# The low parts of the scores in zero-padded tiles of 128 rows

## The chip, the cores and the metric

The kernel runs on one NeuronCore of a Trainium2 chip. The metric is the device time of one execution in microseconds (us). TensorE is called PE below, and its weight loads PEld; VectorE is DVE, ScalarE is ACT, GpSimd is POOL, and SyncE is SP. A difference of 0.2% (2.3 us) is about what a measurement of this kernel can tell from none.

## The reference, cut to what matters

One layer of a hybrid encoder over 512 tokens of 2048 features, all in float32. Half of the mixing heads are differential attention, the other half retention.

```python
u = rmsnorm(h, attn_norm)                    # h: 512 x 2048
z = u @ w_in                                 # 2048 x 7168
rq, rk, rv, rg, dq, dk, dv, dg = split(z)
# retention: 8 heads, keys of 64 features, values of 128
ro = retention(rope(rq), rope(rk) * 64**-0.5, rv)     # (q k^T * decay) v
ro = rmsnorm(ro, ret_gn) * silu(rg)
# differential attention: 8 heads, two scores of 64 features each, values of 128
dq, dk = rmsnorm(dq, diff_qn), rmsnorm(dk, diff_kn)
do = (softmax(q0 k0^T) - lam * softmax(q1 k1^T)) @ dv  # causal by chunks of 64
do = rmsnorm(do, diff_subln) * 0.8 * silu(dg)
h = h + concat(ro, do) @ w_out
out = h + sigmoid(rmsnorm(h, ple_norm) @ w_ple_gate) * (p @ w_ple_proj)
```

## The kernel before, in words

Activations lie feature-major: 128 features on the partitions, 512 tokens in the free dimension. Every float32 operand of a product is split exactly into a high and a low part of type float32r, x = hi + lo, and a product is carried as hi\*hi + hi\*lo + lo\*hi, that is as three matmuls into the same accumulator (`mm3`, L113 to L115). The high part is made by ACT (L106, L109), the low part by DVE (L107, L110).

The projections are cut into chunks of 256 output columns. A chunk goes through 16 k-blocks of 128 features, two k-blocks at a time; such a step is called a slice below. A slice of a feature-major chunk (`fm_products`) has 12 matmuls of 512 columns, one of a values chunk (`v_products`) 24 of 256 columns. A slice is a tick of a clock that the program keeps while it is traced. What follows from a chunk (norms, scores, transposes, values) is set into an agenda some ticks ahead (`after`, `queue_ret`, the tables `QK`, `SCORES`, `TURNS`, `VALUES`, `NORMS`, `RET`), so that these small steps stand between slices of projection products in PE's order. A scheduler then fixes the order of each engine from the traced order and priorities.

**Scores of differential attention** (`stack_q`, `stack_k`, `diff_steps.scores`). A head has two scores of 64 features each. For the first, `qa` holds the high part of q in rows 0 to 63 and its low part in rows 64 to 127, and `k0` holds the high part of k in both halves; one matmul with 128 rows gives hi\*hi + lo\*hi. The remaining term, high part of q by low part of k, is a second matmul into the same bank that takes 64 rows alone: `qs[half, c]` by `kl[half, :L]`. `kl` holds the low part of the first score's k in rows 0 to 63 and that of the second in rows 64 to 127. The second score uses `qb`, `k1` and the other half. For query block b the products have L = 128 (b + 1) columns, so a group of four matmuls (two scores, two products each) has 128, 256, 384 or 512 columns. There are 8 heads of 4 blocks: 32 such groups.

**Scores of retention** (`q_done`, `k_done`, `ret_steps.scores`). `ks` holds the high part of k in one half and the low part in the other, `qd` the high part of q in both; the last term takes the 64 rows of `ks` with the high part and `ql[half]`. A call does two key blocks, of 512 and 384 or of 256 and 128 columns. There are 8 heads of two calls: 16 groups of four matmuls.

In both places every second matmul has 64 rows: 64 at L389 and 32 at L529. `kl` lies in a pool with two buffers, `ql0` and `ql1` in one with a single buffer, a tile for two heads. `squares2` (the squares of a head's output for its norm) takes its tiles for retention from the pool `tmp`, which lives for the whole kernel; the pools `rp` and `rc` live only for the retention stage, and the pool `mixp` (the split operands `mh`, `ml` of the output projection) is opened behind them.

Of the kernel before, what the change touches and what calls it, by code (L numbers as in the profile page):

```python
# [12 lines left out]
F32 = mybir.dt.float32  # L13
# [5 lines left out]
P = 128  # L19
S = 512  # L20
# [18 lines left out]
def f(ap):  # L39
    return ap.bitcast(F32)  # L40
# [3 lines left out]
def tile_layer(  # L44
# [14 lines left out]
):  # L59
    """out^T of one layer.  # L60

    Activations are kept feature-major ([features, tokens]); every product of the
    projections is carried by float32r operands that split float32 exactly into
    x = hi + lo, as hi*hi + hi*lo + lo*hi.
    """
    nc = tc.nc
# [12 lines left out]

# [1 line left out]
    nc.scalar.preload_act_table_set(NORM_SET)  # L81
# [21 lines left out]
    def split(hi, lo, src, gain=None):  # L103
        """hi + lo = src * gain exactly, both float32r."""
        if gain is None:
            nc.scalar.activation(hi, src, AF.Copy)  # L106
            nc.vector.tensor_tensor(lo, src, f(hi), ALU.subtract)  # L107
        else:
            nc.scalar.activation(hi, src, AF.Copy, scale=gain)  # L109
            nc.vector.scalar_tensor_tensor(lo, src, gain, f(hi), ALU.mult, ALU.subtract)  # L110
# [5 lines left out]

# [1 line left out]
    def wchunk(wd, n0, nk, name):  # L118
# [13 lines left out]
    def fm_products(acc, k, nk, wh, wl, mh, ml):  # L132
        """One k-block of [256 features, 512 tokens]: out^T += W^T m."""
        for j in range(2):
            c = slice(j * P, (j + 1) * P)
            mm3(acc[j], wh[:, c], wl[:, c], mh[k], ml[k], k == 0, k == nk - 1)
# [3 lines left out]
    def v_products(acc, k, wh, wl):  # L140
        """One k-block of values of two heads: two [128, token block, 256]."""
        for t in range(4):
            c = slice(t * P, (t + 1) * P)
            o = acc[t // 2][:, (t % 2) * CW:(t % 2 + 1) * CW]
            mm3(o, u_hi[k][:, c], u_lo[k][:, c], wh, wl, k == 0 and t % 2 == 0, k == KB - 1)

    # A job is a generator that traces one slice (two k-blocks) of a chunk's products
    # at a time and, at its end, the evacuation.  An evacuation sets the steps that
    # follow from it some slices ahead, so that the tensor engine has products to do
    # while the other engines prepare a step's operands.  # L150
    agenda = defaultdict(list)
# [49 lines left out]
    def rsqrt(y, z, ss, scale):  # L201
        """y ~ (ss*scale)^-0.5; returns z so that y*(z + 1.5) is it to float32."""
        nc.scalar.activation(y, ss, AF.Ln, scale=scale)
        nc.scalar.activation(y, y, AF.Exp, scale=-0.5)
        nc.scalar.activation(z, y, AF.Square)
        nc.vector.scalar_tensor_tensor(z, ss, -0.5 * scale, z, ALU.mult, ALU.mult)
# [34 lines left out]

    def squares2(src, eps2, name, pool=tmp):
        """As squares, of features in pairs: the low parts lie below the high ones."""
        lo, hi = slice(0, 64), slice(64, P)
# [10 lines left out]
    def normed(t, sq, sel, width, tag, name, cut=None):  # L255
        """t *= rsqrt(mean of squares + eps) over the blocks of sel, 0 where the sum reaches cut."""
        z, sh, sl = sq
# [10 lines left out]

# [1 line left out]
    with ExitStack() as st:  # L270
        xp = st.enter_context(tc.tile_pool(name="xp", bufs=1))
        ssum = xp.tile([P, S], F32, name="ssum")

        # The first two chunks together, a k-block at a time as x arrives; until then
        # products of ones keep the tensor engine's clock up.
        warm = bank("tp", 1, "warm")
# [32 lines left out]

    # lam = exp(lq1.lk1) - exp(lq2.lk2) + 0.2.  The differential output is carried  # L310
    # scaled by c = 1 / max(1, |lam|); its norm undoes the scale.
    lsum = const.tile([P, 2], F32, name="lsum")
# [17 lines left out]
    nc.vector.tensor_scalar(eps_d, eps_d, 2.0**-62, 2.0, ALU.max, ALU.mult)  # L330
    # The reference's sum of squares overflows, and its rsqrt is 0, from here on.
    thr = const.tile([P, 1], F32, name="thr")
# [11 lines left out]

    # ---- differential attention, two heads at a time; on_d holds the gates, then the
    # gated outputs ----
    on_d = [onp.tile([P, S], F32, tag=f"ond{h}", name=f"ond{h}") for h in range(8)]
    A0, A1 = slice(0, 64), slice(64, 128)

    with ExitStack() as st:  # L350
        dp = st.enter_context(tc.tile_pool(name="dp", bufs=2))

        def stack_q(t, h):
# [8 lines left out]
        def stack_k(t, h):  # L362
            k0 = dp.tile([P, S], F32R, tag="k0", name=f"k0{h}")
            k1 = dp.tile([P, S], F32R, tag="k1", name=f"k1{h}")
            kl = dp.tile([P, S], F32R, tag="kl", name=f"kl{h}")
            nc.scalar.activation(k0[A0], t[A0], AF.Copy, scale=g_dk[A0])
            nc.scalar.activation(k1[A1], t[A1], AF.Copy, scale=g_dk[A1])
            nc.vector.tensor_copy(k0[A1], f(k0)[A0])
            nc.vector.tensor_copy(k1[A0], f(k1)[A1])
            nc.vector.scalar_tensor_tensor(kl[A0], t[A0], g_dk[A0], f(k0)[A0], ALU.mult, ALU.subtract)  # L370
            nc.vector.scalar_tensor_tensor(kl[A1], t[A1], g_dk[A1], f(k1)[A1], ALU.mult, ALU.subtract)
            return k0, k1, kl

        def diff_steps(h, pair):
            """Steps of one head: scores and softmax, transposes, values, norm."""
            own = {}
            j = h % 2

            def scores(b):
                qa, qb = pair["q", j]  # L380
                k0, k1, kl = pair["k", j]
                L = (b + 1) * P
                c = slice(b * P, (b + 1) * P)
                sts = small.tile([P, 4], F32, tag="sts", name=f"sts{h}_{b}")
                pt = [dp.tile([P, S], F32, tag=f"p{i}", name=f"p{i}_{h}_{b}") for i in range(2)]
                for i, (qs, ks, half) in enumerate(((qa, k0, A0), (qb, k1, A1))):
                    sc = bank("sc", 2, f"sc{h}_{b}_{i}")[:, :L]
                    nc.tensor.matmul(sc, lhsT=qs[:, c], rhs=ks[:, :L], start=True, stop=False)
                    nc.tensor.matmul(sc, lhsT=qs[half, c], rhs=kl[half, :L], start=False, stop=True)  # L389
                    nc.vector.memset(sc[A0, L - 64:L], NEG)  # L390
# [97 lines left out]

# [1 line left out]
    onr_pool = ctx.enter_context(tc.tile_pool(name="onr", bufs=1))  # L490
    on_r = [onr_pool.tile([P, S], F32, tag=f"onr{h}", name=f"onr{h}") for h in range(8)]

    with ExitStack() as st:
# [20 lines left out]
        def ret_steps(h, qkv):  # L514
            own = {}
            (qd, ql, half), ks = qkv["q", h], qkv["k", h]
            vh, vl = qkv["v"]
            hc = slice((h % 2) * P, (h % 2 + 1) * P)

            def scores(k0):  # L520
# [3 lines left out]
                for kb in (k0, k0 + 1):  # L524
# [3 lines left out]
                    nc.tensor.matmul(sc[:, :N], lhsT=ks[:, c], rhs=qd[:, kb * P:], start=True, stop=False)  # L528
                    nc.tensor.matmul(sc[:, :N], lhsT=ks[half, c], rhs=ql[half, kb * P:], start=False, stop=True)  # L529
                    sf = rp.tile([P, S], F32, tag="sf", name=f"sf{h}_{kb}")  # L530
# [6 lines left out]
            def values(k0):  # L537
# [7 lines left out]
                if k0:  # L545
                    nc.scalar.activation(on_r[h], o, AF.Copy)
                    own["sq"] = squares2(on_r[h], eps2, f"r{h}")

# [14 lines left out]
        for g in range(2):  # L563
            qkv = {}

            def q_done(acc, g=g, qkv=qkv):
                for j in range(2):
                    t = rope(acc[j], f"q{g}_{j}")
                    ql = rc.tile([P, S], F32R, tag=f"ql{j}", name=f"ql{g}_{j}")
                    for i, (half, oth) in enumerate(((A0, A1), (A1, A0))):  # L570
                        qd = rc.tile([P, S], F32R, tag=f"qd{j}{i}", name=f"qd{g}_{j}{i}")
                        nc.scalar.activation(qd[half], t[half], AF.Copy)
                        nc.vector.tensor_copy(qd[oth], f(qd)[half])
                        nc.vector.tensor_tensor(ql[half], t[half], f(qd)[half], ALU.subtract)
                        qkv["q", 4 * g + 2 * j + i] = qd, ql, half

# [30 lines left out]

# [1 line left out]
    mixp = ctx.enter_context(tc.tile_pool(name="mixp", bufs=1))  # L609
# [18 lines left out]

# [1 line left out]
    h_hi, h_lo, h_sb = [], [], []  # L630
    ssum = small.tile([P, S], F32, name="ssum2", bufs=1)

# [20 lines left out]

# [1 line left out]
    p_hi, p_lo = [], []  # L655
# [30 lines left out]
    def output(b, ag, pp, c):  # L686
        """Tokens c of the 128 features of block b; ag holds just those."""
        n = c.stop - c.start
# [14 lines left out]

    # The last chunk a block at a time, its second block by halves of the tokens: less
    # is left to do after the last product.
    pp = ple(7, (("tp", 1), ("o", 1)))
# [20 lines left out]
def _tables():  # L727
    """Rotary cosines and sines and retention decays: they depend on shapes alone."""
    pos = np.arange(S, dtype=np.float32)
# [47 lines left out]
```

## Time and profile before

| | |
|---|---|
| median of 3 runs | 1132.52 us (1132.52 to 1132.53) |
| profiled execution, first to last instruction | 1130.5 us |
| its own time beside the span | as the runs: about 2.0 us lie outside the span |
| PE busy | 1119.7 us (99%), 5668 matmuls |
| PEld busy | 934.6 us (83%), 5668 loads |
| DVE busy | 650.3 us (58%), 1206 instructions |
| ACT busy | 570.1 us (50%), 1049 instructions |
| POOL busy | 0.7 us, 6 instructions |
| DMA | 111.21 MB, 98 GB/s over the span |

The span runs from the first to the last instruction of the program on the core. Busy times are unions of the instructions' durations. Matmuls overlap in the records (a matmul of 512 columns is shown with 389 ns, and the next one starts some 227 ns after it), so PE's busy share does not tell how densely it is fed: for that, the starts of successive matmuls are read from the timeline, and the time from one start to the next is called an interval below. PEclk is the granted clock of TensorE as a share of 2.4 GHz.

### The profile page before, as it was taken

The page shows a single profiled execution, that of the slowest core. Times are in us where ns is not written, and L with a number is a line of the kernel's source. Part 1 is how long each engine was busy: PE and PEld are TensorE (multiplying, and loading weights), DVE is VectorE, ACT ScalarE, POOL GpSimd, SP SyncE. Part 2 cuts the span into 40 slices and gives each one's busy share as a digit, 9 for nine tenths or more (in the row PEclk, how much of TensorE's full clock was granted, in tenths as well). Part 3 has the DMA queues.
Part 4 walks back from the last instruction along what each step waited for, and adds up shares of the span by engine and source line. Part 5 has one row for each costly group of instructions (what it writes and reads, how often), then busy time and mean ns, then how long its engine had stood idle before and what let it go on. Part 6 is the DMA issues. An engine that isn't in the chain of part 4 may idle for free.

```text
span 1130.5 us, 14883 instructions
## 1 busy us (share of the span) xinstructions
PE 1119.7 (99%) x5668; PEld 934.6 (83%) x5668; DVE 650.3 (58%) x1206; ACT 570.1 (50%) x1049; POOL 0.7 (0%) x6
## 2 busy tenths in 40 slices
PE   9999999999999999999999999999999999999998
PEld 7887788788878887899779988888888888888887
DVE  8577579548754875476675467643353354333442
ACT  8467576657665755654575368533333344222230
POOL 0000000000000000000000000000000000000000
PEclk9999999999999999999999999999999999999999
DMA  7422221222222222232222223543332333333341
GB/s 245 127 84 91 75 76 60 74 73 81 87 74 75 76 81 69 88 119 88 90 84 76 89 80 93 186 150 110 95 93 94 96 106 106 112 116 127 109 142 39
DMA packets 104631, 111.21 MB, mean 98 GB/s; under 512 B 4464, under 2 KB 97008, under 8 KB 104560
## 3 DMA queue, kind: packets, MB, share of 16 engines
q1 hardware_dynamic: 101968, 105.55, 30.0%
q10 hardware_dynamic: 2592, 4.72, 1.3%
q8 instruction: 44, 0.72, 0.3%
q14 instruction: 27, 0.22, 0.1%
HBM read 106.06 MB, written 4.19 MB: 98 GB/s over the span
## 4 chain that ended last, share of the span: by engine, by line
PE 94%; ACT 2%; DVE 2%; DMA 0%; issue 0%; SPq 0%; ACTq 0%
PE acc_pg L115 5%; PE acc_pg L114 5%; PE acc_o L115 5%; PE acc_o L114 5%; PE acc_pg L113 5%; PE acc_o L113 5%; PE acc_dg L113 3%; PE acc_rv L113 3%; PE acc_dq L113 3%; PE acc_rv L114 3%; PE acc_rv L115 3%; PE acc_rg L113 3%; PE acc_dg L115 3%; PE acc_dg L114 3%; PE acc_rg L115 3%; PE acc_rg L114 3%
## 5 line engine op out<-in xcount | busy, mean ns | idle before, releaser
L113 PE MATMUL acc_o<-mh,wh_o 128*128 128x512 f32 x256 | 99.6, 389 | 0.0
L114 PE MATMUL acc_o<-ml,wh_o 128*128 128x512 f32 x256 | 99.6, 389 | 0.0
L115 PE MATMUL acc_o<-mh,wl_o 128*128 128x512 f32 x256 | 99.6, 389 | 0.0
L106 ACT ACTIVATE wh_o<-wr_o 128x512 fp32r<-128x512 f32 x64 | 40.4, 631 | 115.8 <-PE acc_o L114 105.4
L107 DVE TENSOR_TENSOR wl_o<-wr_o,wh_o 128x512 fp32r<-128x512 f32 x64 | 44.2, 691 | 92.8 <-ACT wh_o L106 92.8
L115 PE MATMUL acc_pg<-hh,wl_pg 128*128 128x512 f32 x224 | 87.2, 389 | 0.0
L113 PE MATMUL acc_pg<-hh,wh_pg 128*128 128x512 f32 x224 | 87.1, 389 | 0.0
L114 PE MATMUL acc_pg<-hl,wh_pg 128*128 128x512 f32 x224 | 87.1, 389 | 0.0
L106 ACT ACTIVATE wh_pg<-wr_pg 128x512 fp32r<-128x512 f32 x56 | 35.4, 631 | 100.4 <-PE acc_pg L114 80.1
L107 DVE TENSOR_TENSOR wl_pg<-wr_pg,wh_pg 128x512 fp32r<-128x512 f32 x56 | 38.6, 690 | 70.3 <-ACT wh_pg L106 70.3
L113 PE MATMUL acc_rv<-wh_rv,uh 128*128 128x256 f32 x256 | 73.1, 286 | 0.0
L114 PE MATMUL acc_rv<-wl_rv,uh 128*128 128x256 f32 x256 | 72.4, 283 | 0.0
L115 PE MATMUL acc_rv<-wh_rv,ul 128*128 128x256 f32 x256 | 72.4, 283 | 0.0
L114 PEld LDWEIGHTS acc_o<-ml,wh_o 128*128 128x128 f32 x256 | 48.1, 188 | 10.0
L113 PEld LDWEIGHTS acc_o<-mh,wh_o 128*128 128x128 f32 x256 | 48.1, 188 | 10.0
L115 PEld LDWEIGHTS acc_o<-mh,wl_o 128*128 128x128 f32 x256 | 48.1, 188 | 9.8
L113 PE MATMUL acc_dv<-wh_dv,uh 128*128 128x256 f32 x192 | 54.7, 285 | 0.0
L115 PE MATMUL acc_dv<-wh_dv,ul 128*128 128x256 f32 x192 | 54.3, 283 | 0.0
L114 PE MATMUL acc_dv<-wl_dv,uh 128*128 128x256 f32 x192 | 54.3, 283 | 0.0
L113 PE MATMUL acc_dg<-uh,wh_dg 128*128 128x512 f32 x128 | 52.5, 410 | 0.0
L113 PE MATMUL acc_dk<-uh,wh_dk 128*128 128x512 f32 x128 | 50.8, 397 | 0.0
L113 PE MATMUL acc_rg<-uh,wh_rg 128*128 128x512 f32 x128 | 50.6, 395 | 0.0
(311 smaller groups left out, 2976.0 us busy)
## 6 DMA issues: line engine op xcount, KB each, us to landing
wr_o<-w_out SPq DMA_DIRECT2D x32, 512.0 KB, 3.6
wr_pg<-w_gate SPq DMA_DIRECT2D x32, 512.0 KB, 3.6
wr_dk<-w_in SPq DMA_DIRECT2D x16, 512.0 KB, 3.6
wr_dg<-w_in SPq DMA_DIRECT2D x16, 512.0 KB, 3.5
wr_rv<-w_in SPq DMA_DIRECT2D x16, 512.0 KB, 3.5
wr_rg<-w_in SPq DMA_DIRECT2D x16, 512.0 KB, 3.6
wr_dq<-w_in SPq DMA_DIRECT2D x12, 512.0 KB, 3.6
wr_dv<-w_in SPq DMA_DIRECT2D x12, 512.0 KB, 3.6
```

Source lines behind the costliest of these rows:

```text
L106: nc.scalar.activation(hi, src, AF.Copy)
L107: nc.vector.tensor_tensor(lo, src, f(hi), ALU.subtract)
L113: nc.tensor.matmul(out, lhsT=ah, rhs=bh, start=start, stop=False, skip_group_check=True)
L114: nc.tensor.matmul(out, lhsT=ah, rhs=bl, start=False, stop=False, skip_group_check=True)
L115: nc.tensor.matmul(out, lhsT=al, rhs=bh, start=False, stop=stop, skip_group_check=True)
```

## The change

The second product of every score gets all 128 rows. In differential attention `kl` is replaced by four tiles `kz[j][i]` (head parity j, score i), one buffer each, allocated once and set to zero by DVE in the half that is never written again; `stack_k` writes the low part into the other half. The product then takes `qs[:, c]`, the same stationary operand as the first product, by `kz[j][i][:, :L]`. In retention `ql` becomes one tile `qz` per head; POOL sets its idle half to zero in each of the two passes (8 memsets), and the product takes all of `ks`. The 64 rows that are added to the moving operand are zero.

Two things go with it: the tiles of `squares2` for retention come from `rp`, not from `tmp`, and the sum of squares `ssum2` comes from `mixp`, not from `small`. Comments and docstrings were taken out, which moves line numbers: L388 and L389 are L394 and L395 now, L528 and L529 are L534 and L535.

```diff
+        kz = [[dp.tile([P, S], F32R, tag=f"kz{j}{i}", name=f"kz{j}{i}", bufs=1) for i in range(2)]
+              for j in range(2)]
+        for pair in kz:
+            for i, oth in enumerate((A1, A0)):
+                nc.vector.memset(f(pair[i])[oth], 0.0)
...
-            kl = dp.tile([P, S], F32R, tag="kl", name=f"kl{h}")
+            z0, z1 = kz[h % 2]
...
-            nc.vector.scalar_tensor_tensor(kl[A0], t[A0], g_dk[A0], f(k0)[A0], ALU.mult, ALU.subtract)
-            nc.vector.scalar_tensor_tensor(kl[A1], t[A1], g_dk[A1], f(k1)[A1], ALU.mult, ALU.subtract)
-            return k0, k1, kl
+            nc.vector.scalar_tensor_tensor(z0[A0], t[A0], g_dk[A0], f(k0)[A0], ALU.mult, ALU.subtract)
+            nc.vector.scalar_tensor_tensor(z1[A1], t[A1], g_dk[A1], f(k1)[A1], ALU.mult, ALU.subtract)
+            return k0, k1
...
-                    nc.tensor.matmul(sc, lhsT=qs[half, c], rhs=kl[half, :L], start=False, stop=True)
+                    nc.tensor.matmul(sc, lhsT=qs[:, c], rhs=kz[j][i][:, :L], start=False, stop=True)
...
-                    nc.tensor.matmul(sc[:, :N], lhsT=ks[half, c], rhs=ql[half, kb * P:], start=False, stop=True)
+                    nc.tensor.matmul(sc[:, :N], lhsT=ks[:, c], rhs=qz[:, kb * P:], start=False, stop=True)
...
-                    own["sq"] = squares2(on_r[h], eps2, f"r{h}")
+                    own["sq"] = squares2(on_r[h], eps2, f"r{h}", rp)
...
-                    ql = rc.tile([P, S], F32R, tag=f"ql{j}", name=f"ql{g}_{j}")
...
-                        nc.vector.tensor_tensor(ql[half], t[half], f(qd)[half], ALU.subtract)
-                        qkv["q", 4 * g + 2 * j + i] = qd, ql, half
+                        qz = rc.tile([P, S], F32R, tag=f"qz{j}{i}", name=f"qz{g}_{j}{i}")
+                        nc.gpsimd.memset(f(qz)[oth], 0.0)
+                        nc.vector.tensor_tensor(qz[half], t[half], f(qd)[half], ALU.subtract)
+                        qkv["q", 4 * g + 2 * j + i] = qd, qz
...
-    ssum = small.tile([P, S], F32, name="ssum2", bufs=1)
+    ssum = mixp.tile([P, S], F32, name="ssum2")
```

PE at the first scores of the program, block 0 of head 0, before (`acc_dg` is the gate projection of the pair, the last number the columns):

```order
L115 MATMUL acc_dg_1_970<-uh_520,wl_dg_10_1102 128x512
L388 MATMUL sc_0_0_1120<-k_1033,qa_863 128x128
L389 MATMUL sc_0_0_1120<-kl_1035,qa_863 128x128
L388 MATMUL sc_0_1_1126<-k_1034,qb_864 128x128
L389 MATMUL sc_0_1_1126<-kl_1035,qb_864 128x128
L113 MATMUL acc_dg_0_969<-uh_559,wh_dg_12_1139 128x512
```

and the same place after:

```order
L115 MATMUL acc_dg_1_978<-uh_520,wl_dg_10_1108 128x512
L394 MATMUL sc_0_0_1126<-k_1041,qa_871 128x128
L395 MATMUL sc_0_0_1126<-kz_763,qa_871 128x128
L394 MATMUL sc_0_1_1132<-k_1042,qb_872 128x128
L395 MATMUL sc_0_1_1132<-kz_764,qb_872 128x128
L113 MATMUL acc_dg_0_977<-uh_559,wh_dg_12_1145 128x512
```

Nothing moves on PE, here or elsewhere: it has the same 5615 rows in the same order, with other operands at the second product of each score.

ACT at the end of the retention stage, before (`onr`, `sq_r`, `sqb_r`, `sqh_r` and `y_r` belong to the last head's norm, `wh_rg` to the weights of the retention gates, `mh` to the operands of the output projection, `ond` to the finished heads of differential attention):

```order
L546 ACTIVATE onr_5076<-or_6871 128x512
L106 ACTIVATE mh_7072<-rg_0_7104 128x512
L248 ACTIVATE sq_r_6966<-onr_5076 64x512
L249 ACTIVATE sqb_r_6968<-onr_5076 64x512
L106 ACTIVATE mh_7073<-rg_1_7105 128x512
L106 ACTIVATE wh_rg_14_7051<-wr_rg_12_7033 128x512
L251 ACTIVATE sqh_r_6967<-sq_r_6966,eps_92 64x512
L106 ACTIVATE mh_7080<-ond_752 128x512
L106 ACTIVATE mh_7081<-ond_753 128x512
L106 ACTIVATE mh_7082<-ond_754 128x512
L106 ACTIVATE wh_rg_0_7140<-wr_rg_0_7138 128x512
L203 ACT_TABLE_LOAD
```

and after:

```order
L552 ACTIVATE onr_5076<-or_6883 128x512
L248 ACTIVATE sq_r_6978<-onr_5076 64x512
L249 ACTIVATE sqb_r_6980<-onr_5076 64x512
L251 ACTIVATE sqh_r_6979<-sq_r_6978,eps_92 64x512
L106 ACTIVATE wh_rg_14_7063<-wr_rg_12_7045 128x512
L106 ACTIVATE wh_rg_0_7152<-wr_rg_0_7150 128x512
L203 ACT_TABLE_LOAD
L203 ACTIVATE y_r_7022<-ss_r_7020 128x512
L204 ACT_TABLE_LOAD
L204 ACTIVATE y_r_7022<-y_r_7022 128x512
L205 ACTIVATE sq_r_6978<-y_r_7022 128x512
L106 ACTIVATE wh_rg_2_7168<-wr_rg_0_7150 128x512
```

The five splits into `mh` that stood among the last head's squares, and the others that followed them, stand behind that head's norm now; the eight splits of `ond` and the matching low parts on DVE follow in the same way.

POOL, the end of its order, as a difference:

```order
 masks.py:199 AFFINE_SELECT ident<-ident 128x128
-L773 UNCONDITIONAL_BRANCH
-L773 ISA
+L581 MEMSET qz_00_5101 64x512
+L581 MEMSET qz_01_5107 64x512
+L581 MEMSET qz_10_5122 64x512
+L581 MEMSET qz_11_5128 64x512
+L581 MEMSET qz_00_5768 64x512
+L581 MEMSET qz_01_5774 64x512
+L581 MEMSET qz_10_5789 64x512
+L581 MEMSET qz_11_5795 64x512
```

POOL had nothing to do after the constants, and now has the eight memsets of `qz`, four in each pass of retention.

## Rows read from the trace of the kernel before

**Rows 1.** The profile's page: span; chain that ended last; one costly group.
```profile
span 1130.5 us, 14883 instructions
...
PE 94%; ACT 2%; DVE 2%; DMA 0%; issue 0%; SPq 0%; ACTq 0%
...
L106 ACT ACTIVATE wh_o<-wr_o 128x512 fp32r<-128x512 f32 x64 | 40.4, 631 | 115.8 <-PE acc_o L114 105.4
```

**Rows 2.** Line L389 by the tile `kl`: duration min/median/max, first and last start.
```profile
L389 PE MATMUL sc<-kl,qa x32: 324/409/498, 93.9 to 450.1; 64*128 64x128 f32 x8, 64*128 64x256 f32 x8, 64*128 64x384 f32 x8, 64*128 64x512 f32 x8
```

**Rows 3.** Timeline of PE, a score group of 512 columns: start us, duration us.
```profile
134.97 0.39 PE L115 MATMUL acc_dk<-uh,wl_dk 128*128 128x512 f32 x1
135.20 0.39 PE L388 MATMUL sc<-k,qa 128*128 128x512 f32 x1
135.52 0.50 PE L389 MATMUL sc<-kl,qa 64*128 64x512 f32 x1
135.95 0.49 PE L388 MATMUL sc<-k,qb 128*128 128x512 f32 x1
136.37 0.49 PE L389 MATMUL sc<-kl,qb 64*128 64x512 f32 x1
136.79 0.51 PE L113 MATMUL acc_dk<-uh,wh_dk 128*128 128x512 f32 x1
137.13 0.40 PE L114 MATMUL acc_dk<-ul,wh_dk 128*128 128x512 f32 x1
```

**Rows 4.** Timeline of PE: first product of three score groups, second product behind each.
```profile
93.71 0.22 PE L388 MATMUL sc<-k,qa 128*128 128x128 f32 x1
...
94.96 0.39 PE L114 MATMUL acc_dg<-ul,wh_dg 128*128 128x512 f32 x1
...
106.84 0.28 PE L388 MATMUL sc<-k,qa 128*128 128x256 f32 x1
...
108.32 0.39 PE L114 MATMUL acc_dq<-ul,wh_dq 128*128 128x512 f32 x1
...
120.67 0.33 PE L388 MATMUL sc<-k,qa 128*128 128x384 f32 x1
...
122.38 0.40 PE L114 MATMUL acc_dq<-ul,wh_dq 128*128 128x512 f32 x1
```

**Rows 5.** Timeline of PE: values of a head, products of 128 rows.
```profile
172.68 0.34 PE L115 MATMUL od<-ath,vl_dv 128*128 128x384 f32 x1
172.86 0.28 PE L113 MATMUL od<-ath,vh_dv 128*128 128x256 f32 x1
172.98 0.28 PE L114 MATMUL od<-atl,vh_dv 128*128 128x256 f32 x1
...
173.27 0.28 PE L114 MATMUL od<-atl,vh_dv 128*128 128x128 f32 x1
173.39 0.27 PE L115 MATMUL od<-ath,vl_dv 128*128 128x128 f32 x1
```

**Rows 6.** Timeline of PE: two retention groups, first product and second behind each.
```profile
568.35 0.39 PE L528 MATMUL rs<-qd,ks 128*128 128x512 f32 x1
...
570.18 0.40 PE L114 MATMUL acc_rq<-ul,wh_rq 128*128 128x512 f32 x1
...
576.15 0.28 PE L528 MATMUL rs<-qd,ks 128*128 128x256 f32 x1
...
577.51 0.40 PE L114 MATMUL acc_rk<-ul,wh_rk 128*128 128x512 f32 x1
```

**Rows 7.** Timeline of PE: two waits of PE, idle time and releaser in brackets.
```profile
180.98 0.32 PE L389 MATMUL sc<-kl,qb 64*128 64x128 f32 x1 [0.20 <-DVE kl L371]
...
579.99 0.50 PE L113 MATMUL or<-sh,vh_rv 128*128 128x512 f32 x1 [0.92 <-ACT onr L546]
```

**Rows 8.** Windows: busy us of PE, PEld, DVE, ACT, POOL; PEclk; DMA share; GB/s.
```profile
180.00:190.00 10.00, 9.35 (x63) 8.26 (x63) 9.59 (x21) 7.49 (x18) 0.00 (x0) 1.00 0.17 54
```

**Rows 9.** Groups of POOL's instructions: busy us, mean ns of one.
```profile
masks.py:197 POOL MEMSET ident<- 128x128 f32 x1 | 0.2, 204 | 0.3 <-POOLq L767 0.3
```

More of the change, by code (lines that the diff above doesn't have):

```diff
@@ L240, in squares, with squares2 @@
         return sq, sh, sl
-    def squares2(src, eps2, name, pool=tmp):
+    def squares2(src, eps2, name, pool):
         lo, hi = slice(0, 64), slice(64, P)
@@ L380, in scores @@
                 qa, qb = pair["q", j]
-                k0, k1, kl = pair["k", j]
+                k0, k1 = pair["k", j]
                 L = (b + 1) * P
@@ L385, in scores @@
                 pt = [dp.tile([P, S], F32, tag=f"p{i}", name=f"p{i}_{h}_{b}") for i in range(2)]
-                for i, (qs, ks, half) in enumerate(((qa, k0, A0), (qb, k1, A1))):
+                for i, (qs, ks) in enumerate(((qa, k0), (qb, k1))):
                     sc = bank("sc", 2, f"sc{h}_{b}_{i}")[:, :L]
                     nc.tensor.matmul(sc, lhsT=qs[:, c], rhs=ks[:, :L], start=True, stop=False)
-                    nc.tensor.matmul(sc, lhsT=qs[half, c], rhs=kl[half, :L], start=False, stop=True)
+                    nc.tensor.matmul(sc, lhsT=qs[:, c], rhs=kz[j][i][:, :L], start=False, stop=True)
                     nc.vector.memset(sc[A0, L - 64:L], NEG)
@@ L515, in ret_steps @@
             own = {}
-            (qd, ql, half), ks = qkv["q", h], qkv["k", h]
+            (qd, qz), ks = qkv["q", h], qkv["k", h]
             vh, vl = qkv["v"]
```

## The prediction

> **What bounds the kernel now.** I read the page first. The chain of work that ended last is PE for 94% of the span [rows 1], so time is won only where PE's own sequence gets shorter, and time that PE loses anywhere is lost at the end. The busy share of PE (99%) would say that nothing is idle, but the records overlap, so the second view is PE's timeline, read by its starts. In a projection a product of 512 columns is followed by the next after 0.23 us (134.97 to 135.20 in [rows 3]). The granted clock is 1.00, the upper level of 2.4 GHz, where PE also waits [rows 8].
>
> In the score groups the starts are further apart. The product of 64 rows at 135.52 is followed after 0.43 us, the full one at 135.95 after 0.42, the next one of 64 rows after 0.42, and even the first projection product behind the group takes 0.34 us [rows 3]. None of these rows names a releaser, so nothing outside PE is waited for. It is the neighbours of a 64-row product that are slow, on either side. Is it the short width, or that two products add to one bank, or that weights change at each product? The values of a head say no to all three: there 128-row products of 384, 256 and 128 columns, which add to one bank and load weights each time, follow one another after 0.18, 0.12 and 0.12 us [rows 5]. What is left is the step from 128 rows to 64 and back. The tile view has 32 such products with `qa`, eight of each width [rows 2]; 32 more use `qb`, and retention has 32.
>
> The Trainium skill's page "TensorEngine Tiling (Array Packing)" states under Key Properties that a change of the tiling mode, not just of the tile, drains TensorE. By that rule the price is paid on entering and on leaving each 64-row product and goes away altogether with the change; the trace agrees, with 0.42 us in place of 0.23 on both sides.
>
> **The change, part by part.** *The 96 products.* I take a group from the start of its first product to the start of the second projection product behind it, since the slow step out shows there, and subtract what five products would take at the stream's intervals: 0.23 us for 512 columns, 0.18, 0.12 and 0.12 for 384, 256 and 128 [rows 3, 5].
>
> Differential attention, four products and the one behind them: at 512 columns 137.13 - 135.20 = 1.93, less 5 x 0.23 = 1.15, leaves 0.78 [rows 3]; at 384, 122.38 - 120.67 = 1.71, less 4 x 0.18 + 0.23 = 0.95, leaves 0.76; at 256, 108.32 - 106.84 = 1.48, less 0.71, leaves 0.77; at 128, 94.96 - 93.71 = 1.25, less 0.71, leaves 0.54 [rows 4]. Each width comes eight times: 8 x (0.78 + 0.76 + 0.77 + 0.54) = 22.8 us. (One head's block of 256 columns stands in two halves; its two halves count as one.)
>
> Retention: a call with 512 and 384 columns takes 570.18 - 568.35 = 1.83, less 2 x 0.23 + 2 x 0.18 + 0.23 = 1.05, leaves 0.78; a call with 256 and 128 takes 577.51 - 576.15 = 1.36, less 0.71, leaves 0.65 [rows 6]. Eight of each: 8 x 1.43 = 11.4 us.
>
> Together 34.2 us of PE's sequence, if a padded product follows and is followed like the 128-row ones of the values. That it can be no cheaper than they are bounds the gain from above; no gain at all bounds it from below. I take the full gain, because the new product has in every respect (rows, type, weights loaded anew, same bank) the form of the rows that I compare it with.
>
> *What PE gives back by waiting.* PE's order is unchanged, so its products come up to 34 us earlier, and their operands must too. Most are made by DVE and ACT from what PE did shortly before, and move along. Where those two are full, they don't. One place is the start of the second pair's scores: PE waits at 180.98 for DVE's write of `kl` [rows 7], and DVE is busy for 9.59 of the 10 us from 180 to 190 [rows 8]. What the two 128-column groups there save only makes that wait longer: 2 x 0.54 = 1.1 us given back. The other is the first pass of retention, where the products of values at 579.99 wait 0.92 us for ACT's copy `onr` [rows 7], shortly behind a group of 256 and 128 columns: its 0.65 us is given back. Sum 1.75 us. The bounds: nothing, if the operands come earlier as well; above, the first two groups and the third of three pairs, 3 x (0.54 + 0.54 + 0.77) = 5.6, and two groups of retention, 0.65 + 0.78 = 1.4, together 7.0 us. I stay near the lower end because these are the waits that the trace has now, and elsewhere the score products start without a releaser.
>
> *The zeros.* Four memsets of 64 x 512 on DVE at the start, eight on POOL. The nearest row is POOL's memset of 128 x 128, 204 ns [rows 9]; with four times the elements in a partition that makes an estimate of 0.2 to 0.8 us each, up to 3.2 us on DVE and 3.2 us on POOL in each pass. On DVE they stand among the small steps for lam, which nobody needs before the first scores at 93.71 [rows 4]; behind them in DVE's queue are the low parts of the last weights of the x stage, covered by the products that PE still has there. On POOL nothing is queued behind them but the next memset. PE waits for POOL at the first product of each `qz`, eight times; in the first pass a few slices of values lie between, in the second two chunks. Both cost nothing as I count them; with the cover gone, DVE's 3.2 us would be seen once.
>
> *Buffers.* `kz` has one buffer for a head parity, where `kl` had two. `stack_k` of the next pair then waits for the last scores of this one. They are set 21 ticks behind the k chunk, the next writes 24 + 4 = 28 ticks or more, so the wait is over before it begins: 0.
>
> *The moved splits.* `mixp` shares its place with the pools of retention, which are fuller now, and five splits into `mh` that stood among the last head's squares on ACT come after its norm. Each is a split of 128 x 512, 631 ns for the same form [rows 1], so ACT has 5 x 0.63 = 3.2 us less before that norm and as much more behind it, where `wh_rg_4` and `wh_rg_6` are queued behind them. PE waits only for those weights. They are made ahead of use into four buffers, and a slice of 12 products is 12 x 0.23 = 2.8 us of PE; so I count 0, with 3.2 us as the upper bound and a gain of a few tenths (an earlier last norm) as the lower. The new place of `ssum2` and of the squares moves no instruction that PE waits for: 0.
>
> *Sum.* -34.2 + 1.75 = -32.4 us. The profiled span is 1130.5 us [rows 1] and becomes 1098.1; about 2.0 us lie outside it, since the median of the runs is 1132.52 us. Predicted: 1100.1 us.
>
> **The rivals.**
>
> *The other engines become the bound.* PE then gives back what it saves in the first half of every pair's scores, where DVE has norms, stacking and splits of values on top: 4 x 2 x (0.54 + 0.77) = 10.5 us, and the 3.2 us of moved splits. 34.2 - 13.7 = 20.5 us are left: 1112.0 us. For it speaks the window at 180 [rows 8]; against it that DVE is busy for 58% and ACT for 50% of the span, and that PE waits so rarely now.
>
> *The price is not that of the row count.* If it belongs to something that the change keeps (the scores' place between projection products, or the semaphore that the second product sets), the new products keep their intervals: no gain, 1132.5 us. Against it are the 128-row products inside the groups, at 135.95 as slow as their neighbours, and the values' intervals [rows 3, 5].
>
> *Slower: a 64-row product costs half an array.* If the array could run a 64-row product beside its neighbour, the second products would lie beside the first ones now, and after the change each would take its own columns: 16 x (0.23 + 0.18 + 0.12 + 0.12) = 10.4 us and 8 x 0.65 = 5.2 us, together 15.6 us more: 1148.1 us. It decides where a 64-row product is followed sooner than its columns take. The rows show 0.42 us against 0.23 [rows 3], so the products do not lie beside each other here, where a full product stands between any two of them. The same page of the Trainium skill speaks for this rival: under Theoretical Speedup it gives up to 2x for a contraction of 64 rows or fewer. The trace does not agree for this order.
>
> **How the numbers follow.** Forecast 0.85, the other engines 0.09, no gain 0.03, slower 0.03. The range takes the forecast's bounds: at the low end 1132.5 - 34.2 = 1098.3 with nothing given back, and some 1.5 us below it, as the starts have two decimals and 48 groups are summed (48 x 0.03); at the high end 1098.3 + 7.0 for the waits and about half of the 3.2 us of the moved splits, 1107. That leaves out less than 2 in 10. Faster by over 0.2% (2.3 us, about what a measurement of this kernel can tell from no change) 0.94, within it 0.03, slower 0.03.
>
> **What would show it right or wrong.** In the timeline of PE the four products of a score group should start 0.23, 0.18, 0.12 or 0.12 us apart, and the projection product behind them should take 0.23, not 0.34. A 512-column group should span some 1.15 us in place of 1.93. The span should lose about 23 us between the first and the last scores of differential attention and 11 in retention, and nothing behind the retention gates. PE's wait for `kz` at the second pair and for `onr` should each be longer by some tenths. The forecast is wrong if the intervals stay, if PE shows new waits for `wh` or `mh` behind the last retention head, for POOL at L535, or for DVE at many groups.

## The result and the profile after

| | before | after |
|---|---|---|
| median of 4 runs each, side by side | 1132.53 us (1132.52 to 1133.84) | 1099.37 us (1099.03 to 1100.01) |
| profiled execution, first to last instruction | 1130.5 us | 1097.8 us |
| its own time | as the runs | 1099.53 us |

The ratio is 0.9704, with an interval of 0.9690 to 0.9718: the kernel is 33.2 us faster, where 32.4 were predicted (1100.1 us). The span came out 0.3 us from the forecast 1098.1.

The profile's page of the kernel after, span, busy times and the chain that ended last, which answers to [rows 1]:

```profile
span 1097.8 us, 14909 instructions
PE 1085.7 (99%) x5668; PEld 930.9 (85%) x5668; DVE 652.9 (59%) x1210; ACT 569.4 (52%) x1049; POOL 4.9 (0%) x14
...
PE 94%; DVE 3%; ACT 2%; issue 1%; DMA 0%; SPq 0%; ACTq 0%; DVEq 0%
```

PE has the same 5668 products and still holds 94% of the chain: nothing took its place as the bound. Its busy time fell by 34.0 us, the span by 32.7.

**The groups.** PE's timeline of the kernel after: a score group of 512 columns, which answers to [rows 3]; then, in each case as first product and second one behind the group, a group of 128 columns [rows 4], here with the row before the last as well, and the two retention groups [rows 6]. Columns: start us, duration us, engine, line, operation.

```profile
131.78 0.39 PE L394 MATMUL sc<-k,qa 128*128 128x512 f32 x1
132.00 0.39 PE L395 MATMUL sc<-kz,qa 128*128 128x512 f32 x1
132.23 0.39 PE L394 MATMUL sc<-k,qb 128*128 128x512 f32 x1
132.46 0.39 PE L395 MATMUL sc<-kz,qb 128*128 128x512 f32 x1
132.68 0.39 PE L113 MATMUL acc_dk<-uh,wh_dk 128*128 128x512 f32 x1
132.91 0.39 PE L114 MATMUL acc_dk<-ul,wh_dk 128*128 128x512 f32 x1
...
94.39 0.22 PE L394 MATMUL sc<-k,qa 128*128 128x128 f32 x1
...
94.79 0.45 PE L113 MATMUL acc_dg<-uh,wh_dg 128*128 128x512 f32 x1
95.07 0.40 PE L114 MATMUL acc_dg<-ul,wh_dg 128*128 128x512 f32 x1
...
542.36 0.39 PE L534 MATMUL rs<-qd,ks 128*128 128x512 f32 x1
...
543.40 0.39 PE L114 MATMUL acc_rq<-ul,wh_rq 128*128 128x512 f32 x1
...
549.35 0.28 PE L534 MATMUL rs<-qd,ks 128*128 128x256 f32 x1
...
550.04 0.39 PE L114 MATMUL acc_rk<-ul,wh_rk 128*128 128x512 f32 x1
```

The steps of 0.42 us are gone: the four products and the one behind them start 0.22 or 0.23 us apart, as in a projection. The group takes 132.91 - 131.78 = 1.13 us where it took 1.93. The 128-column group takes 0.68 (before 1.25), the retention groups 1.04 (1.83) and 0.69 (1.36). One sign of the prediction is met only in part: behind products of 128 columns the projection product takes 0.28 us (94.79 to 95.07), not 0.23.

**Where along the program.** The tile view gives the first start of every kind of product (durations in ns, then first and last start in us). The kernel before, the first retention scores and the first product with `wh_o`:

```profile
L528 PE MATMUL rs<-qd,ks x32: 276/358/445, 521.1 to 687.5; 128*128 128x512 f32 x8, 128*128 128x384 f32 x8, 128*128 128x256 f32 x8, 128*128 128x128 f32 x8
...
L113 PE MATMUL acc_o<-mh,wh_o x256: 389/389/390, 754.6 to 928.0; 128*128 128x512 f32 x128
```

The same two lines of the kernel after:

```profile
L534 PE MATMUL rs<-qd,ks x32: 220/312/396, 499.5 to 655.2; 128*128 128x512 f32 x8, 128*128 128x384 f32 x8, 128*128 128x256 f32 x8, 128*128 128x128 f32 x8
...
L113 PE MATMUL acc_o<-mh,wh_o x256: 389/389/389, 721.9 to 895.3; 128*128 128x512 f32 x128
```

The first scores start at 94.39 instead of 93.71 [rows 4], 0.7 us late. The first retention scores are 21.6 us early, so differential attention gained 22.3; the first product with `wh_o` is 32.7 early, so retention and its gates gained 11.1. The span ends 32.7 early: nothing was won or lost behind that. The 0.7 us at the start belong to this execution and not to the change: among the traces in which the scores keep their places, the first scores start at 93.3 to 94.4 us where the zeros are written before them (five kernels), and at 93.4 to 94.9 where they are not (four).

**What PE gives back.** The waits of PE in the kernel after: who waited for whom, us in total, times, the longest.

```profile
PE or L113 <- ACT onr L552: 1.6, 1, 1.6
...
PE sc L395 <- DVE kz L377: 0.9, 2, 0.5
PE ss_r L259 <- DVE sqh_r L252: 0.8, 1, 0.8
```

Before, the wait for `onr` was 0.92 us [rows 7], that of `ss_r` 0.9, and those for `kl` 0.6 us in two waits. So two of them grew, the two that the prediction named, and the third stayed. PE's timeline after at these places, where the idle time and its releaser stand in brackets (the first two groups of the second pair, then the products of values):

```profile
174.94 0.22 PE L394 MATMUL sc<-k,qa 128*128 128x128 f32 x1
...
175.88 0.33 PE L395 MATMUL sc<-kz,qb 128*128 128x128 f32 x1 [0.46 <-DVE kz L377]
...
176.21 0.28 PE L114 MATMUL acc_dv<-wl_dv,uh 128*128 128x256 f32 x1
...
182.41 0.33 PE L394 MATMUL sc<-k,qa 128*128 128x128 f32 x1
...
183.72 0.33 PE L395 MATMUL sc<-kz,qb 128*128 128x128 f32 x1 [0.40 <-DVE kz L377]
...
184.17 0.39 PE L114 MATMUL acc_dg<-ul,wh_dg 128*128 128x512 f32 x1
...
553.19 0.50 PE L113 MATMUL or<-sh,vh_rv 128*128 128x512 f32 x1 [1.59 <-ACT onr L552]
```

The same starts in PE's timeline before:

```profile
180.05 0.22 PE L388 MATMUL sc<-k,qa 128*128 128x128 f32 x1
...
181.46 0.28 PE L114 MATMUL acc_dv<-wl_dv,uh 128*128 128x256 f32 x1
...
187.50 0.33 PE L388 MATMUL sc<-k,qa 128*128 128x128 f32 x1
...
189.43 0.39 PE L114 MATMUL acc_dg<-ul,wh_dg 128*128 128x512 f32 x1
```

The first of these groups shrank only from 1.41 to 1.27 us and the second from 1.93 to 1.76, together by 0.31, where two 128-column groups elsewhere shrink by 2 x 0.57 = 1.14: 0.8 us is given back, most of what they saved and not all. From the retention group to the values that wait for `onr`, it was 579.99 - 576.15 = 3.84 us before [rows 6, 7] and is 553.19 - 549.35 = 3.84 after: what that group saved, 0.67 us, is given back to the last hundredth. The windows of the kernel after say why (busy us of PE, PEld, DVE, ACT, POOL; PEclk; DMA share; GB/s); the first answers to [rows 8]:

```profile
175.00:185.00 10.00, 8.91 (x63) 8.03 (x63) 9.59 (x23) 7.48 (x18) 0.00 (x0) 1.00 0.19 54
545.00:555.00 10.00, 8.41 (x43) 6.86 (x42) 6.59 (x12) 9.29 (x16) 0.52 (x1) 1.00 0.16 52
```

DVE is full in the first stretch, ACT in the second. A product saved on PE buys little or nothing where the next operand comes from an engine that has no time left.

**The zeros.** The tile view after, with first and last start: the memsets on DVE and POOL.

```profile
L357 DVE MEMSET kz<- x4: 485/485/485, 36.7 to 40.4; 64x512 f32 x4
...
L581 POOL MEMSET qz<- x8: 518/520/523, 471.5 to 550.0; 64x512 f32 x8
```

About 0.5 us each, inside the estimate of 0.2 to 0.8. No wait of PE names POOL.

### The profile page after: what moved, and what is told of

Same layout as the page of the kernel before. It is cut to its first block, busy times and chain, and to the rows that moved or that the text cites. A ratio compares the mean times of both kernels' runs of the same rounds, so it can differ in the third digit from the quotient of the medians.

```text
span 1097.8 us, 14909 instructions
## 1 busy us (share of the span) xinstructions
PE 1085.7 (99%) x5668; PEld 930.9 (85%) x5668; DVE 652.9 (59%) x1210; ACT 569.4 (52%) x1049; POOL 4.9 (0%) x14
## 4 chain that ended last, share of the span: by engine, by line
PE 94%; DVE 3%; ACT 2%; issue 1%; DMA 0%; SPq 0%; ACTq 0%; DVEq 0%
PE acc_pg L113 5%; PE acc_pg L114 5%; PE acc_pg L115 5%; PE acc_o L115 5%; PE acc_o L113 5%; PE acc_o L114 5%; PE acc_rv L113 3%; PE acc_rv L115 3%; PE acc_rv L114 3%; PE acc_dg L113 3%; PE acc_rg L113 3%; PE acc_dg L114 3%; PE acc_dg L115 3%; PE acc_rg L115 3%; PE acc_rg L114 3%; PE acc_dq L113 3%
```

## The experiments

The theory: each step of PE between products of 128 and of 64 rows costs time, so the gain is that of the groups one by one, less what two full stretches of DVE and ACT give back. Against it stood that the gain comes from the side changes (pools, moved splits, order), that the products' order would do as well as the padding, and that the price is half an array lost or won.

**Differential attention alone.** The kernel after with retention's low parts as they were before (the moved pools stay):

```diff
-                    nc.tensor.matmul(sc[:, :N], lhsT=ks[:, c], rhs=qz[:, kb * P:], start=False, stop=True)
+                    nc.tensor.matmul(sc[:, :N], lhsT=ks[half, c], rhs=ql[half, kb * P:], start=False, stop=True)
```

> Only differential attention is padded (with the changed pools, without which kz does not fit); retention keeps its 64-row products. Theory (a step between 64 and 128 rows costs about 0.2 us each way, PE bounds): 8 x (0.78 + 0.76 + 0.77 + 0.54) = 22.8 less 1.1 given back at the second pair's first scores, so 21.7 us less, about 1110.8 us; the wait of the values on the copy onr stays near the 0.9 us of before, since no group of retention is shorter. Rival (PE runs into the other engines as a whole): clearly less than two thirds of the 33.2 us of the full change, and the wait on onr grows though retention is unchanged.

Measured: 1110.22 us (1109.33 to 1110.43), ratio 0.9800 (0.9786 to 0.9815), a gain of 22.5 us. PE's waits in it:

```profile
PE or L113 <- ACT onr L551: 0.9, 1, 0.9
PE sc L394 <- DVE kz L376: 0.8, 2, 0.5
```

The wait at `kz` has grown nearly as in the kernel after, that for `onr` is what it was: each half of the change gives back at its own place.

**Retention alone.** The kernel before with `qz` in place of `ql`:

```diff
-                    nc.tensor.matmul(sc[:, :N], lhsT=ks[half, c], rhs=ql[half, kb * P:], start=False, stop=True)
+                    nc.tensor.matmul(sc[:, :N], lhsT=ks[:, c], rhs=qz[:, kb * P:], start=False, stop=True)
```

> Only retention is padded; differential attention and the pools are as before. Theory: 8 x 1.43 = 11.4 less 0.65 given back at onr, so 10.8 us less, about 1121.7 us; the waits on kl at the second pair stay at 0.2 and 0.4 us, the wait on onr grows by some 0.7 us. Rival (the moved splits or the pools bring a part of the full gain): less than 10 us here, and the sum of this run and of the one with differential attention alone is short of 33.2 us.

Measured: 1122.42 us (1121.75 to 1122.96), ratio 0.9909 (0.9894 to 0.9924), a gain of 10.3 us. PE's waits in it:

```profile
PE or L113 <- ACT onr L546: 1.6, 1, 1.6
...
PE sc L389 <- DVE kl L371: 0.6, 2, 0.4
```

Now `onr` has the longer wait and `kl` its old one. The two halves add up: 22.5 + 10.3 = 32.8 us, against 33.2 for both. This kernel has no zeros before the scores, and in its trace PE is nevertheless 0.8 us late at the first scores. The kernel with `onr` ahead, further down, has them, and its first scores start at 93.3, 0.4 us early. So the 0.7 us that the kernel after lost there are not the price of the memsets.

**The pools alone.** The kernel before with the two tiles' new places, and so with the moved splits:

```diff
-                    own["sq"] = squares2(on_r[h], eps2, f"r{h}")
+                    own["sq"] = squares2(on_r[h], eps2, f"r{h}", rp)
...
-    ssum = small.tile([P, S], F32, name="ssum2", bufs=1)
+    ssum = mixp.tile([P, S], F32, name="ssum2")
```

> The kernel before with the changed pools alone: the squares of retention in rp, ssum2 in mixp, so that the splits into mh move behind the last retention norm; all 64-row products stay. Theory: these moves lie beside PE's work, 1132.5 us within 0.5. Rival (the moved splits cost, or the squares' own tiles free the first pass of retention): over 1 us one way or the other, by up to 3.2 us.

Measured: 1132.62 us against 1132.62, ratio 0.9998 (0.9989 to 1.0007). The moved splits cost nothing; the 3.2 us that bounded them are not there. At the first scores this kernel, too, without any zeros, is late: by 1.2 us.

**Fewer steps, no padding.** The kernel before with the four products of a group in another order: two full ones, then the two of 64 rows, so that a group has one step in and one out instead of two.

```diff
-                for i, (qs, ks, half) in enumerate(((qa, k0, A0), (qb, k1, A1))):
...
+                for sc, qs, ks in zip(both, (qa, qb), (k0, k1)):
...
+                for sc, qs, half in zip(both, (qa, qb), (A0, A1)):
```

> The kernel before with another order inside each group of four: both 128-row products first, then both 64-row products, which keep their 64 rows. Theory (the price is that of a step between widths): a group has one step in and one out instead of two of each, so half of the 34.2 us goes: about 1115.4 us, with the two 128-row products 0.23 us apart at 512 columns. If the two 64-row products of differential attention, which use different halves of the array, also run beside each other, 8 x (0.23 + 0.18 + 0.12 + 0.12) = 5.2 us more go: about 1110.2 us. Rival (each 64-row product is slow in itself, whatever stands beside it): no gain, 1132.5 us.

Measured: 1110.78 us (1110.72 to 1111.17), ratio 0.9807 (0.9793 to 0.9822): 21.9 us, two thirds of the gain, with the same 64-row products. PE's timeline in it, a group of 512 columns, and a retention group of 512 and 384 columns, first product and second one behind (x2: two products in one row):

```profile
132.04 0.39 PE L388 MATMUL sc<-k,qa 128*128 128x512 f32 x1
132.26 0.39 PE L388 MATMUL sc<-k,qb 128*128 128x512 f32 x1
132.58 0.50 PE L390 MATMUL sc<-kl,qa 64*128 64x512 f32 x1
132.59 0.49 PE L390 MATMUL sc<-kl,qb 64*128 64x512 f32 x1
133.01 0.50 PE L113 MATMUL acc_dk<-uh,wh_dk 128*128 128x512 f32 x1
133.34 0.39 PE L114 MATMUL acc_dk<-ul,wh_dk 128*128 128x512 f32 x1
...
535.32 0.56 PE L528 MATMUL rs<-qd,ks 128*128 128x512 f32 x2
...
536.74 0.39 PE L114 MATMUL acc_rq<-ul,wh_rq 128*128 128x512 f32 x1
```

In retention, where both 64-row products use the same half, the group takes 536.74 - 535.32 = 1.42 us: 0.38 more than the padded 1.04, where two pairs of steps cost 1.83 - 1.04 = 0.79. So **one step in and out costs 0.4 us** at these widths; in the groups of 128 columns, where two pairs cost 1.25 - 0.68 = 0.57, it is 0.29. In differential attention the two use different halves, and they start 0.01 us apart: they do lie beside each other. That group takes 133.34 - 132.04 = 1.30 us, 0.17 more than the padded 1.13: 0.40 for the steps less one product of 0.23.

The Trainium skill's page "TensorEngine Tiling (Array Packing)" states both halves of this: under Key Properties that a change of the tiling mode drains the engine, without a price, and under Theoretical Speedup a gain of up to 2x where a dimension is 64 or smaller. The trace fits both: 0.4 us for a change in and out, and 0.23 us won by the pair; that what takes the 0.4 us is a drain, no run here shows. What decides is which products are neighbours.

**The same order, padded.** The kernel after with two products of `k`, then two of `kz`, so that no step is left to save:

```diff
-                    nc.tensor.matmul(sc, lhsT=qs[:, c], rhs=kz[j][i][:, :L], start=False, stop=True)
+                for sc, qs, kl in zip(both, (qa, qb), kz[j]):
+                    nc.tensor.matmul(sc, lhsT=qs[:, c], rhs=kl[:, :L], start=False, stop=True)
```

> The changed kernel with the same other order inside each group (both high products, then both padded ones). Theory: nothing is left to save, since no step between widths is left: 1099.4 us, within 2 us. Rival (the order itself shortens a group, by keeping products of one bank apart): 2 us or more below 1099.4 us, and then a part of what the order gains with 64-row products is not the step's.

Measured: 1099.60 us (1099.22 to 1099.88), ratio 0.9709 (0.9693 to 0.9725), as the kernel after. The order by itself is worth nothing. The run answers a second question, too: the padded product takes the same stationary operand as the product before it, and could be quick for that. Here the operands alternate, `qa`, `qb`, `qa`, `qb`, and the group of 512 columns still takes 1.13 us (131.51 to 132.64).

**Can the given-back time be had?** Five variants of the kernel after went for the two waits. Their expectations count a wait from start to start, less the usual interval: that for `onr` is then 1.76 us (551.20 to 553.19, less 0.23), where the view of the waits has 1.59. First all scores and what follows from them a slice later:

```diff
-SCORES = ((7, 11, 15, 19), (9, 13, 17, 21))
+SCORES = ((8, 12, 16, 20), (10, 14, 18, 22))
```

with `TURNS`, `VALUES` and `NORMS` one higher, too.

> The changed kernel with the scores, transposes, values and norms of differential attention one tick later. Theory (at the second pair's first scores PE is ahead of DVE, so that what is saved there is given back): the waits of 0.65, 0.35 and 0.58 us there go, since DVE has 2.7 us more, and about 1.5 us are won: 1097.9 us. Rival (PE's order meets other late operands, the scores now stand beside the next pair's norms): the waits come back at other places, no gain, 1099.4 us or more.

Measured: 1098.65 us (1098.05 to 1098.87), ratio 0.9697 (0.9684 to 0.9710), whose interval overlaps that of the kernel after. The wait in the first group is gone, but the second group still waits 0.54 for `k` and 0.40 for `kz`, and a wait of 0.28 at `ss_k` is new.

Then the copy `onr` ahead of the other work on ACT:

```diff
-                    nc.scalar.activation(on_r[h], o, AF.Copy)
+                    with tc.high_priority(offset=AHEAD):
+                        nc.scalar.activation(on_r[h], o, AF.Copy)
```

> The changed kernel with ACT's copy onr of each retention head put ahead by priority. Theory (the 1.76 us wait of the values is for that copy, which stands behind the rope's copies on ACT): the wait falls below 0.5 us and some 1.3 us are won: 1098.1 us. Rival (ACT and DVE are both full there, so that another late operand takes its place): the time stays at 1099.4 us and another wait in the same 20 us grows.

Measured: 1099.44 us (1098.25 to 1100.12), ratio 0.9704 (0.9691 to 0.9717): nothing. One of PE's waits in it:

```profile
PE or L113 <- ACT sh L106: 1.4, 1, 1.4
```

The wait for `onr` is gone and one for `sh`, a split that ACT now does later, stands in its place, at 559.64. The theory that the copy's place in the queue costs the time fell: ACT has too much to do in that stretch.

So the steps of a retention head were set further apart (its first values and its norm a slice later), alone and with the later scores:

```diff
-RET = (0, 2, 2, 5, 7, 4, 3)
+RET = (0, 3, 3, 5, 8, 4, 3)
```

> The changed kernel with retention's table alone spread. Theory: about 2 us less than the changed kernel, 1097.4 us, with the waits on onr and on the squares below 0.5 us each. Rival (the waits move to another operand of the same stretch): within 0.7 us of 1099.4.

Measured: 1098.57 us (1097.83 to 1099.45), ratio 0.9696 (0.9683 to 0.9710).

> The changed kernel with two tables spread: differential attention one tick later, as before, and in retention the first values one tick later (two ticks behind the values of the head before, not one) and the norm one tick later. Theory (what was given back stands at four places where PE is ahead of the other engines, and goes where they get a slice more): the wait of 1.76 us on the copy onr and the one of 0.97 us on the squares behind it fall below 0.5 us each, so 2 us less from retention and 0.8 from the scores: about 1096.5 us. Rival (DVE and ACT are full over the whole 20 us there, so that a tick only moves the wait): no better than 1098.7, the time with late scores alone.

Measured: 1098.18 us (1097.59 to 1098.44), ratio 0.9695 (0.9682 to 0.9708). In both the wait at `ss_r` is gone and the one for `onr` is longer, 2.0 us instead of 1.6.

Last, with later scores and one more slice before the norm, the copy on DVE instead of ACT:

```diff
-RET = (0, 2, 2, 5, 7, 4, 3)
+RET = (0, 2, 2, 5, 8, 4, 3)
...
-                    nc.scalar.activation(on_r[h], o, AF.Copy)
+                    nc.vector.tensor_copy(on_r[h], o)
```

> The changed kernel with differential attention one tick later, the retention norm one tick later, and the copy onr moved from ACT, which is busy for 9.29 of the 10 us around the wait, to DVE, which is busy for 6.59. Theory (at onr the changed kernel gives time back because ACT is full, not because the copy stands late): the wait of 1.76 us falls below 1 us, the one on the squares stays gone: about 1097 us, below the 1098.2 of the kernel with both tables spread. Rival (DVE is as late there, with the rope's products): a wait of 1.5 us or more stays at the first values, 1098.2 us or more.

Measured: 1098.49 us (1097.76 to 1098.92), ratio 0.9700 (0.9687 to 0.9713). PE's longest wait in it behind the start:

```profile
PE ss_r L259 <- DVE sqh_r L252: 2.0, 1, 2.0
```

The wait for `onr` fell to 0.3 us, as the theory had it, but now DVE is late, with the squares. All five came out slower than their theories, by 0.8 to 1.7 us, and wherever a wait went, another came or grew. As far as the windows show, the cause is that ACT is full from 545 to 555 us and DVE behind it (4.84 of the 5 us from 555 to 560 in the last variant), so that time is given back at whichever step comes last. In the median these variants lie between 0.1 us above the kernel after and 1.2 us below it, with intervals that overlap its own; that any of them beats it is not shown by the times.

The traces tell more, because executions differ most at the start: the first product of the first gate projection (`acc_dg`) starts anywhere from 75.99 to 77.92 us. From there to the first product with `wh_o`, PE's timeline of the kernel after:

```profile
77.11 0.39 PE L113 MATMUL acc_dg<-uh,wh_dg 128*128 128x512 f32 x1
...
721.93 0.39 PE L113 MATMUL acc_o<-mh,wh_o 128*128 128x512 f32 x1
```

and that of the variant with both tables changed:

```profile
77.92 0.39 PE L113 MATMUL acc_dg<-uh,wh_dg 128*128 128x512 f32 x1
...
720.85 0.39 PE L113 MATMUL acc_o<-mh,wh_o 128*128 128x512 f32 x1
```

The stretch takes 644.82 and 642.93 us. Where two kernels should not differ, it repeats within 0.2 us: 678.20 in the kernel before and with the pools alone; 644.82 in the kernel after, 644.90 with the padded products in pairs, 644.70 with `onr` ahead. With later scores alone it is 643.93. So in one trace each the later scores win 0.9 us and both tables 1.9. Not all of that is time that the change gave back: PE's wait at `ss_d` for `sq_q`, 1.0 us in the kernel before as well, is 0.4 with later scores. The stretches of the other two variants, 645.37 and 644.44, contain a fall of the clock, described at the end.

## Why the prediction was right

- **The price is the step between row counts.** Right. [rows 3, 5] gave it by exclusion; the reordered kernel shows it directly, since it keeps every 64-row product and half of the steps, and saves half of the price in retention.
- **The size, 34.2 us.** Slightly small. From the groups after: 8 x (0.80 + 0.77 + 0.77 + 0.57) = 23.3 and 8 x (0.79 + 0.67) = 11.7, together 35.0 us. (Groups of 384 columns take 0.94 us after the change, those of 256 take 0.70 to 0.72, one excepted with 0.85.) The starts were read as 0.23 us apart, while five products of 512 columns take 1.13 us, not 1.15. In a 128-column group the first product is followed after 0.06 us (94.39 to 94.45), not 0.12, and the step out takes 0.28: 0.68 in all, not 0.71. The 0.06 could have been seen in the kernel before, where the first 128-column product of the values, between the rows of [rows 5], is followed as soon (173.21 to 173.27).
- **What is given back, 1.75 us.** Right in both places and nearly in size: 0.8 us at the second pair's first scores (1.1 predicted, since the whole saving of two groups was counted) and 0.67 at `onr` (0.65). Choosing the value near the lower end of 0 to 7.0 because only these waits were in the trace held up. 35.0 - 1.5 = 33.5 us is what the groups and the waits give; the trace has 22.3 + 11.1 = 33.4.
- **Zeros, buffers, moved splits: 0.** Right. The memsets take 0.5 us each, and nobody waits for them; the pools alone give 0.9998.
- **The rivals.** That the other engines become the bound holds at those two places and nowhere else: 1.5 us of the 13.7 that it would have cost. That the price is not the row count's is refuted by the timeline. The one that ended slower had a mechanism that holds in part, for two 64-row products of different halves do run side by side when they are neighbours; it was rightly set aside, since a full product stood between any two of them before.

One thing was right by luck in the last digit: the profiled execution's span met the forecast within 0.3 us because 0.7 us lost in the stage at the start, where x is loaded and normed, and 0.8 us more gain in the products cancel.

## What to carry to other kernels

On PE look at the intervals between starts, around a narrow product and on both sides of it, not at busy time or at the count of multiplications: here a lone 64-row product between full ones cost 0.4 us more (0.29 at 128 columns) than the same product padded to 128 rows with zeros. If the zeros can be written once, or on an idle engine, pad; if not, put the narrow products next to each other, those of different halves first of all, and get a part of the gain, two thirds of it here. And before you book a saving on PE, look for the stretches where the engine that feeds it is full: there it comes back as a wait. Setting the steps a slice further apart won some of that back in the traces, at most 1.9 us, too little for the times to show.

## What had not been expected

**Side by side.** The prediction gave the 64-row products nothing for lying beside each other, and the expectation of the reordered kernel left it open. Two of them in different halves, next to each other, started 0.01 us apart (132.58 and 132.59), though each loads its own weights and writes its own bank.

**The clock after a wait.** In the variant with retention's steps further apart, PE waited 1.97 us for `onr`, went on at full rate for 0.8 us, and then ran at the lower of the clock's two levels, 1.2 GHz. PE's timeline of that variant:

```profile
553.80 0.50 PE L113 MATMUL or<-sh,vh_rv 128*128 128x512 f32 x1 [1.97 <-ACT onr L552]
...
556.53 0.63 PE L115 MATMUL acc_rk<-uh,wl_rk 128*128 128x512 f32 x1
556.96 0.63 PE L113 MATMUL acc_rk<-uh,wh_rk 128*128 128x512 f32 x1
```

and a window of it, in the columns as above:

```profile
556.00:558.00 2.00, 2.00 (x6) 1.52 (x6) 1.97 (x5) 1.16 (x2) 0.40 (x1) 0.50 0.57 158
```

The granted clock is 0.50, and products of 512 columns start 0.42 or 0.43 us apart instead of 0.23 until 558.2. The variant with `onr` on DVE shows the same behind its wait of 1.97 us at `ss_r` (0.50 from 559 to 561). The one with later scores as well, and the padded products in pairs, each waited 1.98 us for `onr` and kept a clock of 1.00. So a wait of about 2 us can cost the clock or not; the kernel after, with 1.59 us, keeps 1.00 in its window and in the 3 us behind it. What decides it was not tried. The mean clock of every run hints at how often it happens: in the variant with retention's steps further apart it was 0.998 in the profiled run, the slowest of its five (1099.45 us against 1097.83 to 1098.80), and 1.000 in the other four; with `onr` on DVE it was 0.998 in three runs of five.
